# A transformer layer in float32: the FFN's first strip is entered token half by token half

## The chip, the cores and the metric

The kernel runs on one core of a Trainium2 chip. It issues work to five engines, each of which takes its instructions strictly in order: TensorE (PE in the profile; its weight loads are PEld), VectorE (DVE), ScalarE (ACT), GpSimd (POOL) and SyncE (SP), which issues nearly all DMAs. The metric is the device time of one execution in microseconds, as the median of several runs.

## The reference

One layer (DEPTH 1) of a hybrid diffusion backbone, D_MODEL 2048, over 256 latent tokens with 256 context tokens. A token mixer (gated DeltaNet, Fourier mixing and latent attention, merged by gates) is followed by one output projection and then by a dense SwiGLU FFN of hidden width 5632. Only the end of it matters here:

```
merged = merged + gates[:, :, i] * (branches[i] @ lp["w_branch"][i])
return merged @ lp["w_out"]
...
x = x + mod_l[:, 2] * _rms_norm(y_l, norm_g[l, 1])
h_l = _modulate(_rms_norm(x, norm_g[l, 2]), mod_l[:, 3], mod_l[:, 4])
x = x + mod_l[:, 5] * _rms_norm(_swiglu(h_l, w_ffn_in[l], w_ffn_out[l]), norm_g[l, 3])

def _swiglu(h, w_in, w_out):
    gu = h @ w_in
    return (jax.nn.silu(gu[..., :FF_HIDDEN]) * gu[..., FF_HIDDEN:]) @ w_out
```

All inputs are float32.

## The kernel before, in words

**Numbers.** Each operand of a large matmul is split into a high part, rounded to the matmul's reduced float32 format, and a low part, the rest. ScalarE writes the high part (`hi<-raw` for weights), VectorE or GpSimd the low part (`lo<-raw,hi`). A product is three matmuls (`mm3`, line 302): high x high, high x low, low x high, each 128 x 128 by 256 columns. Small products (`p<-...`) run in plain float32.

**Weights.** Every weight tile is 128 x 1024 (two k-tiles of 512 columns, 512 KB). `reserve` lists the tiles in order of use; `load_to` issues their DMAs into four buffers `raw`; `split_to` makes the high and low part in four pairs of buffers `hi`, `lo`; `get` hands a pair to the matmuls and asks for two tiles ahead.

**Order.** A planner (`Order`, line 100) writes every engine's instructions in an order that it finds from estimated costs: strips of matmuls (`job`) are steps that fill TensorE's time `pe_t`, and side work (`od.add`) is a generator that is taken up when its time is due. `yield 1.0` means: go on 1.0 us later. Background work on the modulation vectors (`bg_tick`, line 788, one step each `bgi` ns, not before `bgt`) is placed between. On the chip the engines keep to this order and wait for one another by semaphores.

**Output projection to FFN (lines 1685 to 1845).** `mT` is the merged branch output, transposed, in two parts. Strips 0 to 2 of `w_out` (512 columns) run token-major (`g_tm`: the tokens of a half are the output's partitions): each weight tile serves both token halves in turn. Strip 3 is cut in two of 256 columns; the second (`last_half`, line 1765) runs all of half 0 and then all of half 1. As soon as a half is done, its norm chain `x1_chain` (line 1728) is added: `rstd` of `y` (VectorE, and a power on GpSimd), the residual sum `y*rstd + x` in four pieces on VectorE, squares of it on ScalarE, a second `rstd`, the store `x1d<-y`, a diagonal `dr` with that `rstd`, and for four groups of four k-tiles (j = 0 to 3): float32 products `p<-dr,y` on TensorE (transpose and scale in one), modulation to `hs`, and the split of `hs` into `h` (high, ScalarE; low, GpSimd for half 0 and VectorE for half 1). For half 0 ScalarE does the modulation, for half 1 VectorE.

The FFN's 11 double strips (`ffn_in`, gate and up, 512 hidden columns) run feature-major (`g_fm`: hidden columns are the partitions, and all 256 tokens stream), so the first strip needs `h` of both halves for each k-tile. `to_hid` splits silu(gate) x up into `hid`, which the last projection `w_ffn_out` reads.

Of the kernel before, what the change touches and what calls it, by code (L numbers as in the profile page):

```python
# [9 lines left out]
F32 = mybir.dt.float32  # L10
# [37 lines left out]
BGI2 = 2700.0  # L48
BGI3 = 3000.0
LIM = 6000.0  # L50
# [195 lines left out]
def kernel(ctx, tc, x, c, ctx_in, c_ctx, w_ada, b_ada, norm_g, w_in, dn_conv, dn_a_log, dn_dt_bias,  # L246
# [52 lines left out]
    def wview(t, kt, n):  # L299
        return t[:, : kt * n].rearrange("p (a b) -> p a b", b=n)  # L300
# [41 lines left out]
    def split_to(i, must=0, eng=None):  # L342
        while wptr[1] < min(i, len(tiles)):
            j = wptr[1]
            load_to(j + 1)
            if j < must:
                od.pe_t = max(od.pe_t, raws[j][1].at)
            elif raws[j][1].at > od.pe_t:
                break
            _, kt, n, o = tiles[j]  # L350
            hi, lo = (wview(wp.tile([P, WE + 2 * FMS], F32R, tag=t, name=t)[:, o:], kt, n) for t in ("hi", "lo"))
            split(hi, lo, raws.pop(j)[0], eng)
            got[j] = (hi, lo, max(act.busy, (eng or dve).busy))
            wptr[1] += 1
            load_to(j + RAWB)
# [14 lines left out]
    for br in (1, 0, 2):  # L370
        for s in range(4):
            wb["br", br, s] = reserve(w_branch[br], 0, s * 512, 512, 8)
    for s in range(3):
        wb["o", s] = reserve(w_out, 0, s * 512, 512, KT)
    for s in range(2):
        wb["o", 3 + s] = reserve(w_out, 0, 1536 + s * 256, 256, KT, 4)
    for s in range(FF // 512):
        for u in range(2):
            wb["f", s, u] = reserve(w_ffn_in, 0, u * FF + s * 512, 512, KT, fm=True)
    for s in range(4):  # L380
# [1294 lines left out]
    job(load_rows, 2, G)  # L1675
    bx["mT"] = [yp.tile([P, KT, 256], F32R, name=f"mT{i}") for i in range(2)]
    y = yp.tile([P, 2, D], F32, name="y")
# [21 lines left out]

    mark(lambda: es_br.close())  # L1700
    for s in range(3):
        job(g_tm, wb["o", s], KT, 512, m_toks, ev_y(y, G, s * 512, 512, s))
    job(g_tm, wb["o", 3], KT, 256, m_toks, ev_y(y, G, 1536, 256, 3), kt=4)
    xr = {}
# [17 lines left out]
    x1d = dram.tile([P, 2, D], F32, name="x1d")  # L1722
    h2 = [hl.tile([P, KT, 256], F32R, tag=f"hl{i}", name=f"h2{i}") for i in range(2)]
    r2 = [None, None]
# [40 lines left out]
    def last_half():  # L1765
        lw = [get(wb["o", 4] + i, 0) for i in range(4)]
        ya = [acc(), acc()]
        ev = ev_y(y, G, 1792, 256, 4)
        for t in range(2):
            for kk in range(KT):  # L1770
                wh, wl = lw[kk // 4]
                mm3(ya[t][:, :256], mT[0][:, kk, tk[t]], mT[1][:, kk, tk[t]], wh[:, kk % 4, :], wl[:, kk % 4, :],
                    kk == 0, kk == KT - 1)
                if kk % 2:
                    yield
            ev(t, ya[t][:, :256])
            x1_done.append(od.add(x1_chain(t), 0.2))

    x1_done = []
    job(last_half)  # L1780
    od.drain()
# [5 lines left out]

    xh2 = [tuple(h2)]
    fx = {}
    es_sg = ExitStack()  # L1790

    def open_hid():
        es_yq.close()
        es_y.close()
        hp = ctx.enter_context(tc.tile_pool(name="hp", bufs=1, side="right", reuse_waits="tile"))
        fx["sgp"] = es_sg.enter_context(tc.tile_pool(name="sgp", bufs=2, reuse_waits="tile"))
        fx["hid"] = [hp.tile([P, NF, 256], F32R, name=f"hid{i}") for i in range(2)]
# [4 lines left out]
    def to_hid(s, sg):  # L1802
        yield 0.0
        hid = fx["hid"]
        split(hid[0][:, s * 4 : s * 4 + 4, :], hid[1][:, s * 4 : s * 4 + 4, :], sg)

    def ffn_in(s):
        if s == 0:
            for t in range(2):
                yield h2_in[t][0]  # L1810
        if s == 1:
            for _ in range(3):
                acc()
        box = []

        def ev_g(b, a):
            if b == 0:
                if s == 0:
                    open_hid()
                box.append(fx["sgp"].tile([P, 4, 256], F32, tag="sgf", name="sgf"))  # L1820
            act.activation(box[0][:, b, :], a[:, :256], AF.Silu)
# [7 lines left out]

        for kk, r in enumerate(g_fm(wb["f", s, 0], KT, xh2, ev_g)):  # L1830
            yield r
            if s == 0 and kk % 4 == 3 and kk < 15:
                for t in range(2):
                    yield h2_in[t][kk // 4 + 1]
# [135 lines left out]
```

## Time and profile before

| | us |
|---|---|
| three timed runs | 2012.37, 2017.92, 2030.83 |
| median | 2017.92 |
| profiled execution | 2000.15 |
| its span (first to last instruction) | 1998.3 |
| TensorE busy in the span | 1912.4 |
| VectorE, ScalarE, GpSimd busy | 1258.1, 912.9, 53.9 |

TensorE is the engine that sets the time. A difference of a few microseconds has to be looked for in the stretches in which it waits, or in which its matmuls take longer than elsewhere: the timeline of one engine gives, in brackets, how long the engine was idle before a row and who released it; the windows give each engine's busy time and the clock that TensorE was granted (1.00 is 2.4 GHz, 0.50 is 1.2 GHz). Output projection and step into the FFN lie at 1148 to 1280 us, the FFN's input strips end at 1744, the last projection fills the rest.

### The profile page before, as it was taken

The numbers are of one execution on the slowest core, as the hardware profiler recorded it, in microseconds if no ns is written. First come the engines' busy times: TensorE is split into PE (matmuls) and PEld (weight loads), VectorE is DVE, ScalarE is ACT, GpSimd is POOL, SyncE is SP. The second block draws the span as 40 slices with busy tenths as digits, with TensorE's granted clock in tenths as the row PEclk, the third lists the DMA queues.
The fourth block names the chain that finished last, engine by engine and source line by source line (L and its number), as shares of the span: only waits on it lengthen the run. The fifth ranks groups of instructions, "written<-read, shape, count | busy, mean of one in ns | idle before, by whom it ended". The sixth has DMA issues, their size and how long they took to land.

```text
span 1998.3 us, 41454 instructions
## 1 busy us (share of the span) xinstructions
PE 1912.4 (96%) x17359; PEld 1879.8 (94%) x17359; DVE 1258.1 (63%) x1891; ACT 912.9 (46%) x1492; POOL 53.9 (3%) x64
## 2 busy tenths in 40 slices
PE   5999989999999999999999999899999999999998
PEld 4899988999999899999999998899999999999998
DVE  3444758887866567656766876777755454554444
ACT  3213776564444345445444344544444444434442
POOL 1000010010000000000000000100000000000000
PEclk8999999999999899999999999899999999999999
DMA  9997667778998689855544887688876666676664
GB/s 298 290 291 190 229 185 230 262 227 256 310 306 267 198 289 292 277 167 176 161 146 135 293 285 274 222 299 278 273 218 197 191 196 194 180 269 194 193 195 141
DMA packets 310680, 463.45 MB, mean 232 GB/s; under 512 B 41224, under 2 KB 128670, under 8 KB 307805
## 3 DMA queue, kind: packets, MB, share of 16 engines
q1 hardware_dynamic: 310156, 459.81, 73.6%
q8 instruction: 136, 2.23, 0.5%
q0 software_dynamic: 336, 1.00, 0.2%
q14 instruction: 52, 0.42, 0.1%
HBM read 432.39 MB, written 28.35 MB: 231 GB/s over the span
## 4 chain that ended last, share of the span: by engine, by line
PE 49%; DVE 2%; ACT 1%; DMA 1%; issue 1%; POOL 0%; SPq 0%; DVEq 0%; POOLq 0%; ACTq 0%
PE acc L95 45%; PE p L95 4%; DMA raw<-in_w_ffn_out_dram 1%; ACT hi L95 0%; DVE lo L95 0%; DVE hs L95 0%; DVE aacc L95 0%; ACT hs L95 0%; DVE yo L95 0%; DVE dr L95 0%; DVE mg L95 0%; ACT h L95 0%; DVE yhl L95 0%; ACT sq L95 0%; POOL h L95 0%
## 5 line engine op out<-in xcount | busy, mean ns | idle before, releaser
L95 DVE TENSOR_TENSOR lo<-raw,hi 128x1024 fp32r<-128x1024 f32 (+2 forms) x534 | 648.8, 1219 | 464.6 <-ACT hi L95 459.6
L95 ACT ACTIVATE hi<-raw 128x1024 fp32r<-128x1024 f32 (+2 forms) x536 | 562.4, 1055 | 584.4 <-PE acc L95 462.2
L95 PE MATMUL acc<-h,hi 128*128 128x256 f32 x2816 | 481.3, 277 | 0.7 <-ACT h L95 0.4
L95 PEld LDWEIGHTS acc<-h,hi 128*128 128x128 f32 x2816 | 425.2, 188 | 1.3 <-ACT h L95 0.7
L95 PE MATMUL acc<-hi,hTl 128*128 128x256 f32 (+1 forms) x2112 | 413.0, 289 | 2.1 <-ACT ai L95 2.1
L95 PE MATMUL acc<-h,lo 128*128 128x256 f32 x1408 | 389.3, 277 | 0.7 <-DVE lo L95 0.7
L95 PEld LDWEIGHTS acc<-hi,hTl 128*128 128x128 f32 x2112 | 337.1, 191 | 2.9 <-ACT ai L95 2.5
L95 PE MATMUL acc<-lo,hTl 128*128 128x256 f32 (+1 forms) x1056 | 299.5, 284 | 0.0
L95 PEld LDWEIGHTS acc<-h,lo 128*128 128x128 f32 x1408 | 264.9, 188 | 1.0 <-DVE lo L95 1.0
L95 PE MATMUL acc<-hi,hid 128*128 128x256 f32 x1408 | 240.3, 276 | 0.5 <-ACT hi L95 0.5
L95 PEld LDWEIGHTS acc<-hi,hid 128*128 128x128 f32 x1408 | 211.9, 188 | 1.0 <-ACT hi L95 0.7
L95 PEld LDWEIGHTS acc<-lo,hTl 128*128 128x128 f32 x1056 | 201.8, 191 | 0.3 <-DVE lo L95 0.2
L95 PE MATMUL acc<-lo,hid 128*128 128x256 f32 x704 | 194.4, 276 | 0.9 <-DVE lo L95 0.9
L95 DVE SCALAR_TENSOR_TENSOR aacc<-araw,sc,aacc 128x512 f32<-128x512 f32 x240 | 179.3, 747 | 4.8 <-DMA araw<-in_w_ada_dram 3.7
L95 PE MATMUL acc<-hi,yhl 128*128 128x256 f32 x768 | 144.6, 285 | 7.1 <-DVE yhl L95 3.7
L95 PEld LDWEIGHTS acc<-lo,hid 128*128 128x128 f32 x704 | 132.2, 188 | 1.3 <-DVE lo L95 1.1
L95 PE MATMUL acc<-hTl,hi 128*128 128x256 f32 x640 | 125.4, 287 | 7.1 <-ACT kr L95 3.6
L95 PEld LDWEIGHTS acc<-hi,yhl 128*128 128x128 f32 x768 | 121.3, 191 | 8.9 <-DVE yhl L95 4.3
L95 PEld LDWEIGHTS acc<-hTl,hi 128*128 128x128 f32 x640 | 100.5, 195 | 10.7 <-ACT hi L95 4.0
L95 PE MATMUL acc<-lo,yhl 128*128 128x256 f32 x384 | 107.7, 281 | 0.0
L95 PE MATMUL acc<-hTl,lo 128*128 128x256 f32 x320 | 91.2, 285 | 1.2 <-DVE lo L95 1.2
L95 PE MATMUL acc<-hi,mT 128*128 128x256 f32 x512 | 89.5, 279 | 0.0
(306 smaller groups left out, 2517.5 us busy)
## 6 DMA issues: line engine op xcount, KB each, us to landing
raw<-in_w_in_dram SPq DMA_DIRECT2D x176, 512.0 KB
raw<-in_w_ffn_in_dram SPq DMA_DIRECT2D x176, 512.0 KB
araw<-in_w_ada_dram SPq DMA_DIRECT2D x148, 512.0 KB
raw<-in_w_ffn_out_dram SPq DMA_DIRECT2D x88, 512.0 KB
raw<-in_w_branch_dram SPq DMA_DIRECT2D x48, 512.0 KB
xt<-in_w_ada_dram SPq DMA_DIRECT2D x44, 512.0 KB
raw<-in_w_out_dram SPq DMA_DIRECT2D x32, 512.0 KB
hk<-qkvd SPq DMA_DIRECT2D x8, 1024.0 KB
```

The costliest lines, as they stand in the source:

```text
L95: return f(*a, **k)
```

## The change

Strip 3 of `w_out` is no longer cut: `last_o` runs its 512 columns for half 0 and then for half 1, and keeps its eight weight tiles for the second pass. Four of them lie in the four `hi`/`lo` pairs, the first four in buffers named `kept` in the space that `h` takes later (`hold`, in tags hl0, hl1). The FFN's first gate strip (`ffn_first`) runs token-major in the same way: all of half 0, waiting only for half 0's `h`, then all of half 1. Its tiles 0 to 3 lie in `hi`/`lo`, tiles 4 to 7 in `kept` buffers in the space of `mT`. A limit `wlim` lets a tile be refilled one tile behind the last use. The first up strip is token-major too; the product is transposed back (`turn_hid`, eight transposes) just before the last double strip. In `x1_chain` the delays are other, `dr` is made by ScalarE, modulation and low parts alternate between engines by j for both halves, and the store of `x1` is issued at the end. Background work is pushed back by 60 us at the step (`bgt`), and its spacing BGI3 is 2700 instead of 3000. The gated strip `sgf` has one buffer instead of two.

```diff
-BGI3 = 3000.0
+BGI3 = 2700.0
...
     def split_to(i, must=0, eng=None):
-        while wptr[1] < min(i, len(tiles)):
+        while wptr[1] < min(i, len(tiles), wlim[0]) or wptr[1] in held and wptr[1] < f0:
...
-            hi, lo = (wview(wp.tile([P, WE + 2 * FMS], F32R, tag=t, name=t)[:, o:], kt, n) for t in ("hi", "lo"))
+            if j in held:
+                hi, lo = (wview(v, kt, n) for v in held.pop(j)())
+            else:
+                hi, lo = (wview(wp.tile([P, WE + 2 * FMS], F32R, tag=t, name=t)[:, o:], kt, n) for t in ("hi", "lo"))
...
-    for s in range(3):
+    for s in range(4):
         wb["o", s] = reserve(w_out, 0, s * 512, 512, KT)
-    for s in range(2):
-        wb["o", 3 + s] = reserve(w_out, 0, 1536 + s * 256, 256, KT, 4)
...
+    o3, f0 = wb["o", 3], wb["f", 0, 0]
+    wlim[0] = f0
...
+    def hold(pool_, tags, j0):
+        kept = {}
+
+        def part(q):
+            if q // 2 not in kept:
+                kept[q // 2] = pool_.tile([P, 4 * WE], F32R, tag=tags[q // 2], name="kept")
+            v, o = kept[q // 2], q % 2 * 2 * WE
+            return v[:, o : o + WE], v[:, o + WE : o + 2 * WE]
+
+        for q in range(4):
+            held[j0 + q] = lambda q=q: part(q)
...
     def x1_chain(t):
         r = sum_rstd(ssy[:, t, :])
-        yield 1.0
+        yield 0.3
...
-        yield 0.0
+        yield -1.5
         r2 = sum_rstd(ssx[:, t, :])
-        od.dma(out=x1d[:, t, :], in_=y[:, t, :])
-        if t:
-            split_to(wb["f", 0, 0] + 2, eng=pool)
-        yield 1.0
+        yield 0.5
         dr = yp.tile([P, P], F32, tag=f"dr{t}", name="dr")
-        vmul(dr, ident, r2)
+        amul(dr, ident, r2)
         yield ada_in[3]
         yield ada_in[4]
+        bgt[0] = od.pe_t + 60000.0
         for j in range(4):
...
-                if t == 0:
+                if j % 2 == 0:
                     act.activation(o, i_, AF.Identity, bias=sh, scale=sc1)
...
-            split(h2[0][:, js, tk[t]], h2[1][:, js, tk[t]], hs, (pool, dve)[t])
+            split(h2[0][:, js, tk[t]], h2[1][:, js, tk[t]], hs, pool if j % 2 else dve)
             od.fire(h2_in[t][j])
             yield 0.0
...
+        od.dma(out=x1d[:, t, :], in_=y[:, t, :])
+
+    def last_o():
+        lw = []
         ya = [acc(), acc()]
-        ev = ev_y(y, G, 1792, 256, 4)
+        ev = ev_y(y, G, 1536, 512, 3)
         for t in range(2):
             for kk in range(KT):
...
+                i = kk // KC
+                if t == 0 and kk % KC == 0:
+                    lw.append(get(o3 + i, 3))
+                wh, wl = lw[i]
+                mm3(ya[t], mT[0][:, kk, tk[t]], mT[1][:, kk, tk[t]], wh[:, kk % KC, :], wl[:, kk % KC, :], kk == 0,
+                    kk == KT - 1)
+                if t and kk % KC == 1 and i >= 5:
+                    wlim[0] = f0 + i - 4
+                    split_to(f0 + 8, eng=pool if i == 5 else None)
+                yield
+            if t:
+                hold(yp, ("mT0", "mT1"), f0 + 4)
+                wlim[0] = f0 + 8
+            ev(t, ya[t])
+            split_to(f0 + 4 * t, f0 + 4 * t)
             x1_done.append(od.add(x1_chain(t), 0.2))
...
+    def turn_hid(t, sg):
+        pt = pst(t)
+        transpose4(pt, sg[:, t, :])
+        hid, ptv = fx["hid"], pt.rearrange("p (b t) -> p b t", b=4)
+        split(hid[0][:, 0:4, tk[t]], hid[1][:, 0:4, tk[t]], ptv)
+
+    def ffn_first():
+        lw = []
+        ga = [acc(), acc()]
+        for t in range(2):
+            for kk in range(KT):
+                i = kk // KC
+                if kk % 4 == 0:
+                    yield h2_in[t][kk // 4]
+                if t == 0 and kk % KC == 0:
+                    lw.append(get(f0 + i, 1))
...
+                if t and kk % KC == 1:
+                    wlim[0] = f0 + 8 + min(i + 1, 4)
+                    split_to(wlim[0])
+                yield
...
+        yield from g_tm(wb["f", 0, 1], KT, 512, [(h2[0], h2[1], s) for s in tk], ev_up)
...
+    job(ffn_first)
+    for s in range(1, FF // 512):
         job(ffn_in, s)
```

ScalarE's order before, at the norm of the two halves (`sq,ssy<-acc` closes a half's output strip, `sq,ssx<-y` are the squares of its residual sum, `hs` its modulation, `h` its rounding, `hi<-raw` a weight tile's high part; numbers tell the buffers apart):

```order
L95 ACTIVATE sq,ssx<-y 128x512 x4
L95 ACTIVATE sq,ssy<-acc 128x256
L95 ACTIVATE hs<-p_15221,modT 128x128 x4
L95 ACTIVATE h_13519<-hs 128x4x128
L95 ACTIVATE sq,ssx<-y 128x512 x4
L95 ACTIVATE hs<-p_15245,modT 128x128 x4
L95 ACTIVATE h_13519<-hs 128x4x128
L95 ACTIVATE hi<-raw 128x1024 x2
```

The same place after the change, on ScalarE (`kept<-raw` is the high part of a held tile, here tiles 4 to 6 of the FFN's first gate strip):

```order
L95 ACTIVATE hi<-raw 128x1024 x2
L95 ACTIVATE h_15172<-hs 128x4x128
L95 ACTIVATE hi<-raw 128x1024
L95 ACTIVATE sq,ssy<-acc 128x512
L95 ACTIVATE hi<-raw 128x1024
L95 ACTIVATE hs<-p_15245,modT 128x128 x4
L95 ACTIVATE h_15172<-hs 128x4x128
L95 ACTIVATE sq,ssx<-y 128x512 x4
L95 ACTIVATE h_15172<-hs 128x4x128
L95 ACTIVATE kept<-raw 128x1024 x3
L95 ACTIVATE dr<-cs,rstd 128x128
```

Half 1's closing square now stands behind three weight tiles' high parts, where it stood right behind half 0's squares; and the held tiles 4 to 6 stand behind the squares of half 1's residual sum and behind half 0's last rounding.

VectorE after the change, from the low part of half 0's first `h` on:

```order
L95 TENSOR_TENSOR h_15173<-hs,h_15172 128x4x128
L95 TENSOR_TENSOR lo<-raw,hi 128x1024
L95 TENSOR_SCALAR hs<-p_15206,modT 128x128 x4
L95 TENSOR_TENSOR lo<-raw,hi 128x1024
L95 TENSOR_TENSOR y<-acc,G 128x512
L95 TENSOR_TENSOR lo<-raw,hi 128x1024
L95 TENSOR_TENSOR h_15173<-hs,h_15172 128x4x128
L95 TENSOR_REDUCE ss<-ssy 128x1
L95 TENSOR_SCALAR rstd<-ss 128x1
L95 SCALAR_TENSOR_TENSOR y<-y,rstd,xr 128x512 x4
L95 TENSOR_SCALAR hs<-p_15312,modT 128x128 x4
L95 TENSOR_TENSOR kept<-raw,kept 128x1024 x2
```

Half 1's product with the gate, `y<-acc,G`, stands behind the low part of the FFN's tile 2, and its norm behind tile 3 and half 0's third `h`; before, nothing but half 0's own chain stood there.

TensorE just before the last double strip, after the change (`sgt` is the first strip's gated product):

```order
L95 MATMUL acc<-h_15172,lo 128x256
L95 MATMUL p_20426<-cs,sgt 128x128 x4
L95 MATMUL p_20433<-cs,sgt 128x128 x4
L95 MATMUL acc<-h_15172,hi 128x256
L95 MATMUL acc<-h_15173,hi 128x256
```

Before, no float32 product stood between the last `p<-dr,y` and the end of the FFN's input strips; now these eight transposes do.

## Rows read from the trace of the kernel before

**Rows 1.** Page: busy us and share of TensorE; chain that ended last, by engine.

```profile
PE 1912.4 (96%) x17359; PEld 1879.8 (94%) x17359; DVE 1258.1 (63%) x1891; ACT 912.9 (46%) x1492; POOL 53.9 (3%) x64
...
PE 49%; DVE 2%; ACT 1%; DMA 1%; issue 1%; POOL 0%; SPq 0%; DVEq 0%; POOLq 0%; ACTq 0%
```

**Rows 2.** Windows: length, busy PE, PEld, DVE, ACT, POOL, granted clock, DMA share, GB/s.

```profile
1205.00:1210.00 5.00, 5.00 (x46) 5.00 (x46) 3.34 (x5) 2.12 (x2) 0.00 (x0) 1.00 0.91 305
...
1245.00:1250.00 5.00, 1.78 (x10) 1.46 (x8) 2.19 (x5) 4.94 (x15) 1.28 (x1) 0.84 0.98 329
1250.00:1255.00 5.00, 0.46 (x2) 0.46 (x3) 2.38 (x2) 4.15 (x8) 4.69 (x4) 0.50 0.10 40
...
1260.00:1265.00 5.00, 5.00 (x32) 5.00 (x32) 2.81 (x6) 2.17 (x4) 1.27 (x1) 0.68 0.45 133
```

**Rows 3.** Timeline of TensorE at the step: start, length, operation, [idle before, releaser].

```profile
1239.37 0.28 PE L95 MATMUL acc<-hi,mT 128*128 128x256 f32 x1
1242.10 4.68 PE L95 MATMUL p<-dr,y 128*128 128x128 f32 x24 [2.45 <-DVE dr L95]
1254.54 3.78 PE L95 MATMUL p<-dr,y 128*128 128x128 f32 x16 [7.76 <-DVE dr L95]
1258.74 0.58 PE L95 MATMUL acc<-h,hi 128*128 128x256 f32 x1 [0.42 <-ACT h L95]
...
1265.65 1.06 PE L95 MATMUL p<-dr,y 128*128 128x128 f32 x8
1266.46 0.48 PE L95 MATMUL acc<-h,hi 128*128 128x256 f32 x2
...
1274.15 0.40 PE L95 MATMUL acc<-h,hi 128*128 128x256 f32 x2
...
1274.51 0.40 PE L95 MATMUL acc<-h,hi 128*128 128x256 f32 x2
...
1279.37 0.39 PE L95 MATMUL acc<-h,lo 128*128 128x256 f32 x1 [0.75 <-DVE lo L95]
```

**Rows 4.** Timeline of ScalarE at the step.

```profile
1234.10 0.38 ACT L95 ACTIVATE sq<-acc 128x256 f32<-128x256 f32 x1 [5.35 <-PE acc L95]
...
1245.11 0.63 ACT L95 ACTIVATE h<-hs 128x512 fp32r<-128x512 f32 x1
...
1248.10 1.47 ACT L95 ACTIVATE hs<-p,modT 128x128 f32<-128x128 f32 x4
...
1250.14 1.99 ACT L95 ACTIVATE hi<-raw 128x1024 fp32r<-128x1024 f32 x2
```

**Rows 5.** Timeline of VectorE at the step.

```profile
1242.18 2.74 DVE L95 SCALAR_TENSOR_TENSOR y<-y,rstd,xr 128x512 f32<-128x512 f32 x4 [0.23 <-POOL rstd L95]
...
1252.13 2.36 DVE L95 TENSOR_SCALAR dr<-cs,rstd 128x128 f32<-128x128 f32 x1 [2.11 <-POOL rstd L95]
...
1261.72 1.45 DVE L95 TENSOR_TENSOR lo<-raw,hi 128x1024 fp32r<-128x1024 f32 x1 [1.65 <-ACT hi L95]
1263.10 1.36 DVE L95 TENSOR_SCALAR hs<-p,modT 128x128 f32<-128x128 f32 x4
...
1266.10 1.23 DVE L95 TENSOR_TENSOR lo<-raw,hi 128x1024 fp32r<-128x1024 f32 x1 [0.25 <-ACT hi L95]
```

**Rows 6.** Timeline of GpSimd at the step.

```profile
1251.54 0.55 POOL L95 TENSOR_TENSOR rstd<-rstd,nhalf 128x1 f32<-128x1 f32 x1
1252.05 4.65 POOL L95 TENSOR_TENSOR lo<-raw,hi 128x1024 fp32r<-128x1024 f32 x2
...
1260.82 1.27 POOL L95 TENSOR_TENSOR h<-hs,h 128x512 fp32r<-128x512 f32 x1 [2.89 <-ACT h L95]
```

**Rows 7.** Timeline of TensorE, transposes in the output projection.

```profile
1154.69 0.60 PE L95 MATMUL p<-cs,mg 128*128 128x128 f32 x4
```

**Rows 8.** Windows of 50 us without a wait of TensorE.

```profile
500.00:550.00 50.00, 50.00 (x427) 50.00 (x426) 43.10 (x69) 21.84 (x27) 2.69 (x2) 1.00 0.96 308
...
1450.00:1500.00 50.00, 50.00 (x443) 50.00 (x443) 24.88 (x24) 21.62 (x24) 0.00 (x0) 1.00 0.73 221
```

More of the change, by code (lines that the diff above doesn't have):

```diff
@@ L320 @@
     wptr = [0, 0]
+    wlim, held = [1 << 30], {}
     def reserve(w, k0, c0, n, nk, kt=KC, fm=False):
@@ L1675 @@
     job(load_rows, 2, G)
-    bx["mT"] = [yp.tile([P, KT, 256], F32R, name=f"mT{i}") for i in range(2)]
+    bx["mT"] = [yp.tile([P, KT, 256], F32R, tag=f"mT{i}", name=f"mT{i}") for i in range(2)]
     y = yp.tile([P, 2, D], F32, name="y")
@@ L1698, with open_o @@
     m_toks = [(mT[0], mT[1], s) for s in tk]
-    mark(lambda: es_br.close())
-    for s in range(3):
+    def hold(pool_, tags, j0):
[7 more added lines that the diff above has]
+            held[j0 + q] = lambda q=q: part(q)
+    def open_o():
+        es_br.close()
+        hold(hl, ("hl0", "hl1"), o3)
+    mark(open_o)
+    for s in range(2):
         job(g_tm, wb["o", s], KT, 512, m_toks, ev_y(y, G, s * 512, 512, s))
-    job(g_tm, wb["o", 3], KT, 256, m_toks, ev_y(y, G, 1536, 256, 3), kt=4)
     xr = {}
@@ L1722 @@
     x1d = dram.tile([P, 2, D], F32, name="x1d")
-    h2 = [hl.tile([P, KT, 256], F32R, tag=f"hl{i}", name=f"h2{i}") for i in range(2)]
-    r2 = [None, None]
+    h2 = []
     h2_in = [[Event() for _ in range(4)] for _ in range(2)]
@@ L1760, in x1_chain @@
             js = slice(j * 4, j * 4 + 4)
-            split(h2[0][:, js, tk[t]], h2[1][:, js, tk[t]], hs, (pool, dve)[t])
+            if not h2:
+                h2.extend(hl.tile([P, KT, 256], F32R, tag=f"hl{i}", name=f"h2{i}") for i in range(2))
+            split(h2[0][:, js, tk[t]], h2[1][:, js, tk[t]], hs, pool if j % 2 else dve)
             od.fire(h2_in[t][j])
             yield 0.0
-    def last_half():
-        lw = [get(wb["o", 4] + i, 0) for i in range(4)]
+        od.dma(out=x1d[:, t, :], in_=y[:, t, :])
+    def last_o():
+        lw = []
         ya = [acc(), acc()]
-        ev = ev_y(y, G, 1792, 256, 4)
+        ev = ev_y(y, G, 1536, 512, 3)
         for t in range(2):
             for kk in range(KT):
[L1771 to L1776, printed above, removed]
+                i = kk // KC
[13 more added lines that the diff above has]
+            split_to(f0 + 4 * t, f0 + 4 * t)
             x1_done.append(od.add(x1_chain(t), 0.2))
     x1_done = []
-    job(last_half)
+    job(last_o)
     od.drain()
@@ L1786 @@
         return
-    xh2 = [tuple(h2)]
+    xh2 = []
     fx = {}
@@ L1805, in to_hid, with ev_up @@
         split(hid[0][:, s * 4 : s * 4 + 4, :], hid[1][:, s * 4 : s * 4 + 4, :], sg)
+    def turn_hid(t, sg):
[13 more added lines that the diff above has]
+                    lw.append(get(f0 + i, 1))
+                wh, wl = lw[i]
+                mm3(ga[t], h2[0][:, kk, tk[t]], h2[1][:, kk, tk[t]], wh[:, kk % KC, :], wl[:, kk % KC, :], kk == 0,
+                    kk == KT - 1)
+                if t and kk % KC == 1:
+                    wlim[0] = f0 + 8 + min(i + 1, 4)
+                    split_to(wlim[0])
+                yield
+        wlim[0] = 1 << 30
+        bgt[0] = od.pe_t
+        open_hid()
+        xh2.append(tuple(h2))
+        sg = fx["sgp"].tile([P, 2, 512], F32, tag="sgt", name="sgt")
+        for t in range(2):
+            act.activation(sg[:, t, :], ga[t], AF.Silu)
+        fx["turn"] = lambda: [turn_hid(t, sg) for t in range(2)]
+        def ev_up(t, a):
+            dve.tensor_tensor(out=sg[:, t, :], in0=sg[:, t, :], in1=a, op=ALU.mult)
+        yield from g_tm(wb["f", 0, 1], KT, 512, [(h2[0], h2[1], s) for s in tk], ev_up)
     def ffn_in(s):
-        if s == 0:
-            for t in range(2):
-                yield h2_in[t][0]
         if s == 1:
@@ L1813, in ffn_in @@
                 acc()
+        if s == FF // 512 - 1:
+            fx["turn"]()
         box = []
@@ L1828, in ev_up @@
                 od.add(to_hid(s, sg))
[L1830 to L1834, printed above, removed]
+        yield from g_fm(wb["f", s, 0], KT, xh2, ev_g)
         yield from g_fm(wb["f", s, 1], KT, xh2, ev_up)
-    for s in range(FF // 512):
+    job(ffn_first)
+    for s in range(1, FF // 512):
         job(ffn_in, s)
```

9 lines of the change are left out of this document (4 added, 5 removed).

## The prediction

> **What bounds the kernel now.** I read the page's busy shares first: TensorE is at work 96% of the span, and its matmuls are most of the chain that ended last [rows 1]. So only time in which TensorE waits, or runs at its lower clock, can be won. The windows show where that is at the place of the change: from 1245 to 1265 us the granted clock is between 0.50 and 0.84, while it is 1.00 at 1205 [rows 2]. The timeline of TensorE names the waits [rows 3]. The last matmul of the output projection ends at 1239.65 (1239.37 + 0.28); TensorE waits 2.45 us for the diagonal `dr` of token half 0, 7.76 for that of half 1, 0.42 for `h`, and 0.75 for a weight tile's low part at 1279.37.
>
> What does this step cost? From 1239.65 to 1279.37 are 39.7 us. In them stand the 8 groups of norm products, 0.81 us each at the full clock (1265.65 to 1266.46), so 6.5, and ten k-tiles of 12 FFN matmuls and two more, 122. One takes 0.113 us (50 us / 443 records [rows 8]), so 13.8. The loss is 39.7 - 20.3 = 19.4 us: 11.4 of waits and 8.0 of half clock (the groups of `dr` take 4.68 us for 24 records and 3.78 for 16, instead of 2.4 and 1.6), slower pace and hand-overs. These 19.4 us, 1.0% of the time, are all that the change can win there.
>
> **What the change removes.** The last 512 columns of `w_out` now run token half by token half, 96 matmuls or 10.9 us each instead of 5.4, so half 0's norm runs beside 10.9 us of matmuls. The first gate strip of the FFN also runs by halves, so that it can start before half 1's norm is done. If every cover held, the 19.4 us would go. I walk the new order from Z, the end of half 0's last output matmul, with durations from the rows.
>
> *Half 0.* Before, its chain takes 8.0 us from the square of its sums at 1234.10 [rows 4] to the first product at 1242.10 [rows 3]. In that time TensorE has 66 matmuls queued ahead of the first group, 7.5 us: it waits 0.5. Thirty matmuls (3.4) and three groups (2.4) later, at Z + 13.8, it enters the FFN.
>
> *First tile.* Scaling by ScalarE (1.47) and rounding (0.63) of the first four k-tiles end at Z + 11.0, the high part of the first FFN tile (1.0, half of 1.99) at 12.0 [rows 4]; its low part is on GpSimd, 2.33 (half of 4.65 [rows 6]), to 14.4. TensorE waits 0.6.
>
> *Third tile.* VectorE's order is: low part of tile 1, scaling of the second four k-tiles (1.36), low part of tile 2 (1.23) [rows 5]. VectorE's subtraction beside a GpSimd operation took 1.45 instead of 1.23, and one `dr` 2.36 beside the two GpSimd subtractions [rows 5, 6]. So I let tile 1 wait until GpSimd ends: 14.4 + 1.2 = 15.6; scaling to 17.0, rounding 17.6, high part of tile 2 18.6, low part 19.8. TensorE asks for it at 17.0: it waits 2.9. The Trainium skill, "SBUF — State Buffer", section "SBUF: two separate sides", says that the pair of ports that VectorE and GpSimd share is an exclusive lock, which also a VectorE operation with two SBUF inputs has to wait for; the rows agree (1.45 for 1.23). Without it, tile 1 would end at 14.2 and the wait would be 1.5: the sum would be 1.4 us less.
>
> *Fifth tile, the large one.* The square of half 1's sums stands on ScalarE behind the high part of tile 2, and its product with the gate on VectorE behind that tile's low part. So half 1's norm, whose matmuls end at Z + 13, begins at 19.8. Then come tile 3 (to 21.6), the third scaling and rounding (23.2), the root on GpSimd (0.55 [rows 6]; 24.2), four residual sums (2.74 [rows 5]; 26.9), the fourth scaling and rounding (28.9), and only then the high part of tile 4, whose turn on ScalarE is behind all of these: 29.9, the low part 31.1. TensorE is through with tile 3 at 23.4. It waits 6.5 and 1.2.
>
> *After it.* Tile 7 stands behind half 1's `dr`, scaling and rounding: 3.0. The last GpSimd subtraction of `h` costs 0.7. The waits are 0.5 + 0.6 + 2.9 + 7.7 + 3.0 + 0.7 = 15.4 us.
>
> *Clock.* Before, the clock fell to half after a wait of 2.45 us and again in one of 7.76, and came back some 8 us after work resumed [rows 2, 3]. A wait of 6.5 and one of 3.0 lie near these, so I expect it to fall again. I take the 8.0 us that were no wait before, less 2.3 for the first 24 records, whose slowness stood inside the 7.76: 5.7. The ends are 0 (no fall) and 8.0.
>
> *Added at the end of the FFN's input.* Eight transposes turn the token-major strip. Four took 0.60 [rows 7]: 1.2 us. Their two evacuations have a strip of 43 us ahead of their reader.
>
> *At nothing:* the 1 MB residual stores move behind the norm on SyncE's queue, and the data are read back only after the FFN; VectorE's `dr` goes to ScalarE (inside the 8.0). One buffer fewer for the gated strip: its reader is done some 7 conversions before the next strip writes; without that cover, each of ten strips would wait for one conversion, about 1 us. BGI3 of 2700 instead of 3000 and the pause of the modulation work by 60 us move VectorE work that has 450 us of FFN to finish in. The loads: 15 tiles in a row, four raw buffers. At 305 GB/s, the rate of the stage before [rows 2], a 512 KB tile takes 1.7 us, and tile 4's load has 14 us between the freeing of its buffer (Z + 14.4) and its turn.
>
> **Sum.** Removed 19.4; added 15.4 + 5.7 + 1.2 = 22.3; difference +2.9 us, with the bounds of the clock term and of the lock -4.2 to +5.2. The hand-overs in my walk are taken rather long, and I round to +2. The profiled execution took 2000.15 us, span 1998.3; by the sum it becomes 2002. The three timed runs lie 12 to 31 us above it, median 2017.92. So **2020 us**, likeliest range 2010 to 2030 with the spread of the runs. A difference of less than 1%, 20 us, can't be told from none here.
>
> **Rivals.**
>
> *The matmuls stay at the slower pace (slower).* After groups in another number format (`p<-cs`, `p<-dr`) the matmuls come at either of two spacings, at a clock of 1.00: 427 records in 50 us at one place, 443 at the other, 0.117 and 0.113 us [rows 8]. In the timeline the slower one (three matmuls in 0.36 us, 1274.15 to 1274.51) still holds long after the last `dr` group; behind the wait of 0.75 at 1279.37 the FFN is at the faster one [rows 3, 8]. After the change, 3720 matmuls follow the last group before the next one. If the spacing falls on the slow side, and no wait follows that resets it (my 0.7 is a weak one), they cost 3720 x 0.0042 = 16 us: 2036. For: the toss falls about evenly in this trace. Against: a wait follows in my walk. Chance 0.18. The Trainium skill, "TensorE: Matmul & The Clock Gate", section "Back-to-back issue gap", gives one spacing at the full clock, N / 2.4 + 2.5 ns, 109 ns for 256 columns. By that this rival does not exist and its 0.18 would go to the wash; the trace differs, with two spacings, both above it.
>
> *The waits are mostly hidden (faster).* If ScalarE and VectorE reach half 1's chain at its due time, the wait of 7.7 and the fall of the clock go: 2020 - 7.7 - 5.7 = 2007. For: the code asks for tiles at a time that a plan finds early enough. Against: engines work in order, and the rows before show ScalarE at 4.9 of 5 us in 1245 to 1250 [rows 2]. Chance 0.18.
>
> *The weights come late, so the halves step in on nothing held.* Then each of the eight first tiles waits for its load instead. Price: two or three loads of 1.7, 4 us more, 2024. Against: see the loads above. Chance 0.08.
>
> The wash keeps 0.56. The range for 8 in 10 reaches from the hidden case less the runs' spread, 2001, to the slow pace, 2036. Faster by over 1% (below 1998): a third of the hidden case's lower tail and little else, 0.07. Slower by over 1% (above 2038): nearly half of the slow pace, and a tail of the wash, 0.10. Within 1%: 0.83.
>
> **What would show it.** Right: TensorE waits for `dr` of half 0 under 1 us, enters the FFN without the wait of 7.76, and then waits 6 to 8 us at the fifth tile with ScalarE's high part as releaser, the clock at 0.50 for some windows, and 440 records per 50 us in the FFN. Wrong: a step with under 10 us of waits, a clock of 1.00 throughout it, or 425 records per 50 us.

## The result, and the profile after

The changed kernel takes 2021.31 us (median of 20 runs), the kernel before 2003.1 (20 runs beside them). The ratio is 1.0075, 95% interval 1.0054 to 1.0095: slower by 0.75%, some 15 us. The predicted time, 2020 us, is 1.3 us away, and that is luck: its base, the median of the three runs shown (2017.92), was 14.8 us too high, and the predicted difference, +2, was 13 us too small (16 by the medians, which lie 18.2 us apart). The three were among the six slowest of the 20. Over all its runs in this study the kernel before lies in two groups, near 2002 and near 2018 us; what speaks for a cause is shown below.

The profiled execution took 2008.61 us, span 2006.8, against 2000.15 and 1998.3 before. On the page of the changed kernel TensorE's share and the chain answer to [rows 1]: still 96% and half of the chain, with 12 us more of busy time.

```profile
PE 1924.5 (96%) x17367; PEld 1891.3 (94%) x17367; DVE 1258.2 (63%) x1887; ACT 912.7 (45%) x1489; POOL 53.6 (3%) x63
...
PE 49%; DVE 1%; ACT 1%; DMA 1%; issue 1%; POOL 0%; SPq 0%; DVEq 0%; POOLq 0%; ACTq 0%
```

TensorE's waits in the step into the FFN (1222 to 1285 us), grouped by who was waited for: total, times, longest.

```profile
PE acc L95 <- ACT kept L95: 7.4, 2, 5.6
PE acc L95 <- DVE kept L95: 1.8, 2, 0.9
PE acc L95 <- DVE lo L95: 1.1, 1, 1.1
PE acc L95 <- ACT hi L95: 1.0, 1, 1.0
PE acc L95 <- POOL lo L95: 0.3, 1, 0.3
```

That is 11.6 us; before it was 11.4 [rows 3]. The two waits for `dr` are gone, and waits of the same size for the FFN's weight tiles stand in their place. The timeline of TensorE after, which answers to [rows 3], has them one by one:

```profile
1221.04 0.39 PE L95 MATMUL acc<-lo,mT 128*128 128x256 f32 x1 [0.87 <-DVE lo L95]
...
1222.44 5.92 PE L95 MATMUL acc<-kept,mT 128*128 128x256 f32 x48
1228.19 0.29 PE L95 MATMUL acc<-hi,mT 128*128 128x256 f32 x1
...
1230.25 1.13 PE L95 MATMUL p<-dr,y 128*128 128x128 f32 x8
...
1237.05 0.39 PE L95 MATMUL acc<-lo,h 128*128 128x256 f32 x1 [0.29 <-POOL lo L95]
...
1241.02 0.39 PE L95 MATMUL acc<-hi,h 128*128 128x256 f32 x1 [0.99 <-ACT hi L95]
1242.51 0.39 PE L95 MATMUL acc<-lo,h 128*128 128x256 f32 x1 [1.10 <-DVE lo L95]
...
1251.93 0.58 PE L95 MATMUL acc<-kept,h 128*128 128x256 f32 x1 [5.58 <-ACT kept L95]
1253.42 5.27 PE L95 MATMUL acc<-kept,h 128*128 128x256 f32 x23 [0.90 <-DVE kept L95]
...
1262.90 0.39 PE L95 MATMUL acc<-kept,h 128*128 128x256 f32 x1 [1.77 <-ACT kept L95]
1264.16 0.86 PE L95 MATMUL acc<-kept,h 128*128 128x256 f32 x5 [0.87 <-DVE kept L95]
...
1279.87 0.29 PE L95 MATMUL acc<-hi,h 128*128 128x256 f32 x1
```

From the end of half 0's output matmuls (1222.44) to the end of the gate strip (1279.87) are 57.4 us. In them stand 288 matmuls (32.5 at 0.113) and eight groups of `dr` (6.5): a loss of 18.4 us where the kernel before lost 19.4. The step is a wash, as forecast. One price in it stood in no term: the 48 matmuls that stream a `kept` tile from 1222.44 to 1228.19 come 0.120 us apart, not 0.113.

What is new lies behind it. Windows of the changed kernel (columns as in [rows 2]), which answer to [rows 8]: two of 18 us in the first up strip, which is token-major, and in the second double strip, which is feature-major; two of 50 us later in the FFN and in `w_ffn_out`.

```profile
1282.00:1300.00 18.00, 18.00 (x161) 18.00 (x161) 11.81 (x13) 7.25 (x7) 0.00 (x0) 1.00 0.88 306
1303.00:1321.00 18.00, 18.00 (x155) 18.00 (x155) 12.76 (x15) 6.37 (x6) 0.00 (x0) 1.00 0.88 291
...
1650.00:1700.00 50.00, 50.00 (x427) 50.00 (x426) 24.57 (x23) 20.66 (x23) 0.00 (x0) 1.00 0.66 189
1800.00:1850.00 50.00, 50.00 (x444) 50.00 (x443) 24.00 (x21) 20.81 (x23) 0.00 (x0) 1.00 0.61 194
```

TensorE is busy for all of each window, at a granted clock of 1.00, and waits for nothing; yet 155 matmuls come in 18 us instead of 161, 427 in 50 instead of 444. The slow spacing begins at 1301.65, with the first feature-major matmul of the FFN, and lasts to the transposes at 1708.80: 3456 matmuls x (50/427 - 50/443 = 0.0042 us) = 14.6 us. A window also counts the matmuls that only reach into it, so this is a little low, as is every product with 0.0042 below: by their starts the 3456 came in 407.15 us, 0.1178 us apart, and the 192 of the up strip (1279.87 to 1301.65) 0.1134 apart, which makes 15.2 us. Busy shares and waits can't show this; the count in a window does.

The profiled executions differ by 8.5 us: 15.2 for the spacing, 1.5 for new waits in the last output strip (the 0.87 at 1221.04 and smaller ones), 1.0 for the transposes, -1.0 for the step, and -7.1 because the work ahead of all this took that much less in this execution (the matmul behind the same transposes of `mg` starts at 1132.97 instead of 1140.07). -1.1 is not assigned.

### The profile page after: what moved, and what is told of

It reads as the page before. It is cut to its first block, busy times and chain, and to the rows that moved or that the text cites. A ratio compares the mean times of both kernels' runs of the same rounds, so it can differ in the third digit from the quotient of the medians.

```text
span 2006.8 us, 41458 instructions
## 1 busy us (share of the span) xinstructions
PE 1924.5 (96%) x17367; PEld 1891.3 (94%) x17367; DVE 1258.2 (63%) x1887; ACT 912.7 (45%) x1489; POOL 53.6 (3%) x63
## 4 chain that ended last, share of the span: by engine, by line
PE 49%; DVE 1%; ACT 1%; DMA 1%; issue 1%; POOL 0%; SPq 0%; DVEq 0%; POOLq 0%; ACTq 0%
PE acc L95 45%; PE p L95 4%; DMA raw<-in_w_ffn_out_dram 1%; ACT hi L95 1%; DMA raw<-in_w_out_dram 0%; ACT hs L95 0%; DVE kept L95 0%; DVE hs L95 0%; DVE lo L95 0%; DVE y L95 0%; DVE yo L95 0%; DVE mg L95 0%; ACT h L95 0%; DVE yhl L95 0%; ACT kept L95 0%
## 5 line engine op out<-in xcount | busy, mean ns | idle before, releaser
L95 DVE TENSOR_TENSOR lo<-raw,hi 128x1024 fp32r<-128x1024 f32 (+2 forms) x527 | 641.3, 1222 | 472.0 <-ACT hi L95 470.1
L95 ACT ACTIVATE hi<-raw 128x1024 fp32r<-128x1024 f32 (+2 forms) x528 | 553.2, 1054 | 581.0 <-PE acc L95 478.7
L95 PE MATMUL acc<-h,hi 128*128 128x256 f32 x2560 | 450.7, 281 | 0.0
L95 PEld LDWEIGHTS acc<-h,hi 128*128 128x128 f32 x2560 | 394.4, 190 | 0.0
L95 PE MATMUL acc<-h,lo 128*128 128x256 f32 x1280 | 359.5, 281 | 0.0
L95 PEld LDWEIGHTS acc<-h,lo 128*128 128x128 f32 x1280 | 240.4, 188 | 0.0
L95 PE MATMUL acc<-hTc,hi 128*128 128x256 f32 x384 | 79.6, 290 | 5.9 <-ACT ai L95 5.9
```

What stands on the lines that cost most here:

```text
L95: return f(*a, **k)
```

## The experiments

Theory P: the loss is the slow spacing in the FFN, left behind by the step's last float32 products because no wait resets it. Theory S: the loss is the step itself, and the spacing a chance of one execution. The windows of 18 us above later gave theory R (roles): the slow spacing comes in where matmuls go over from token-major to feature-major without a pause. e11 and e12 test it. The times of e1 to e4 were taken beside the same runs of the kernel before, and so were those of e5 to e7, of e8 and e9, and of e11 and e12; between these sets, the ratios are what can be compared.

**e1_again**, the changed kernel untouched.

> The changed kernel once more, untouched, as the mark for the other three of this call. Theory P (pace): the loss of about 15 us against the kernel before lies in some 3700 FFN matmuls that come 0.0045 us further apart (0.118 for 0.113 us) because nothing behind the last float32 products of the step resets their spacing. Then this execution again has about 425 records per 50 us between 1300 and 1700 us, and 443 only behind the eight transposes near 1709. Theory S (step): the loss lies in the step itself (the waits of 5.86 and 2.05 us and the stretch at half clock), and the spacing of one profiled execution was a toss that comes out either way in another. Time by both: 1.0054 to 1.0095 of the kernel before, near 2018 us.

Measured: 2018.12 us, ratio 1.0040 (1.0010 to 1.0070). The FFN was slow again, and this time `w_ffn_out` too, which was fast in the first profile. A window of e1 there:

```profile
1850.00:1900.00 50.00, 50.00 (x426) 50.00 (x426) 23.44 (x20) 19.67 (x22) 0.00 (x0) 1.00 0.60 186
```

That is 1967 matmuls x 0.0042 = 8.3 us more, and this execution took 2029.62 us. In that stage the spacing comes out either way.

**e2_turn_early**, the same work with the float32 transposes 350 us earlier:

```diff
-        if s == FF // 512 - 1:
+        if s == 2:
             fx["turn"]()
```

> The changed kernel with its eight float32 transposes (p<-cs,sgt) at the start of the third double strip instead of the last; no work is added. P: the group throws the spacing over some 350 us earlier, so about 3080 more matmuls run at 0.113 us, 3080 x 0.0045 = 13.9 us less than the changed kernel, near 2004 us, and 443 records per 50 us from about 1370 us on. S: no change, within 2 us of the changed kernel, and 425 or 443 records per 50 us with no step at the transposes.

Measured: 2006.69 us, ratio 0.9983 (0.9958 to 1.0008), 11.4 us below e1, taken beside it. Windows of e2 ahead of the transposes (1357.86) and behind them:

```profile
1315.00:1333.00 18.00, 18.00 (x155) 18.00 (x154) 12.42 (x14) 6.86 (x7) 0.00 (x0) 1.00 0.87 284
...
1400.00:1450.00 50.00, 50.00 (x444) 50.00 (x443) 37.40 (x45) 23.17 (x25) 0.00 (x0) 1.00 0.87 288
```

The step's waits are those of the changed kernel, to 0.1 us. Moving eight small products took most of the loss away, so it is the spacing and not the step.

**e3_before_group**, the kernel before with a useless float32 group (`f32_group`: four `pe.transpose` of a constant):

```diff
         if s == 1:
             for _ in range(3):
                 acc()
+            f32_group()
```

> The kernel before with four float32 transposes of a constant (0.6 us, their result is read by nobody) at the start of the FFN's second double strip, where it is at the fast spacing. P: the group throws it to the slow one for the 3840 matmuls of ten double strips, 3840 x 0.0045 = 17.3 us, with the group's own 0.6 about 18 us slower than the kernel before (ratio 1.009), 425 records per 50 us up to 1744 us. S: 0.6 us slower, ratio 1.0003, 443 records.

Its profiled execution, 2024.07 us, was fast ahead of the group at 1316.04 and slow behind it:

```profile
1290.00:1315.00 25.00, 25.00 (x223) 25.00 (x222) 17.27 (x20) 12.89 (x15) 0.00 (x0) 1.00 1.00 343
1350.00:1400.00 50.00, 50.00 (x427) 50.00 (x427) 33.13 (x38) 21.37 (x23) 0.00 (x0) 1.00 0.82 263
```

But the median is 2006.35, ratio 1.0014 (0.9976 to 1.0053): 4 of its 12 runs lie at 2015.61 or above, 8 at 2010.98 or below. A miss for P: a float32 group can throw the spacing, as this execution shows, but the times do not show that it always does. (Of the kernel before's own 35 runs beside it, 8 lie above 2012.)

**e4_wait**, the changed kernel with one long wait and no float32 product:

```diff
+                if s == 1:
+                    wait_once(a)    # four copies on ScalarE, then a matmul that needs the last
```

> The changed kernel with one forced wait of TensorE and no float32 product: at the end of the second double strip four copies in a row on ScalarE (128 x 256 each, into a part of hid that is written over later), and one matmul in the large matmuls' own format that waits for the last. P, as the wait of 0.75 us reset the spacing in the kernel before: TensorE waits 1.2 to 1.8 us near 1364 us and then comes at 0.113 us, 3080 x 0.0045 = 13.9 less 1.5: 12 us faster than the changed kernel. P in a narrower form, that only float32 products throw the spacing: 1.5 us slower than the changed kernel, still 425 records behind the wait. S: 1.5 us slower.

Measured: 2017.85 us, ratio 1.0032 (1.0000 to 1.0064). TensorE of e4 waited 2.66 us and stayed slow, as the window behind shows:

```profile
1354.80 0.39 PE L95 MATMUL p<-hid 128*128 128x256 f32 x1 [2.66 <-ACT hid L95]
```

```profile
1400.00:1450.00 50.00, 50.00 (x427) 50.00 (x426) 36.35 (x44) 21.24 (x25) 0.00 (x0) 1.00 0.85 278
```

A wait does not by itself reset the spacing, and the premise of P in its wide form falls.

**e5_map**, `f32_group` at the start of each of nine double strips:

```diff
-        if s == FF // 512 - 1:
+        if s < FF // 512 - 1:
+            f32_group()
+        else:
             fx["turn"]()
```

> The changed kernel with four float32 transposes of a constant (0.6 us, read by nobody) at the start of each of the second to tenth double strips, so that one execution shows nine tosses. P: the spacing changes at these groups and nowhere between them. Counted over the six traces so far, a group of four threw slow matmuls to the fast spacing in 164 of 165 cases and fast ones to the slow in 132 of 208. So a slow strip (384 matmuls at 0.118 us) is always followed by a fast one (0.113), a fast one by a slow one about six times in ten; some four of the nine are slow: 2018 - 5 x 384 x 0.0045 = 8.6 + 9 x 0.6 = 5.4: 2015 us. S: 5.4 us more than the changed kernel, 2023, and one spacing throughout.

Measured: 2018.82 us, ratio 1.0049 (1.0017 to 1.0081), 4 us above P. Windows of 20 us, one in each of four double strips in a row:

```profile
1410.00:1430.00 20.00, 20.00 (x179) 20.00 (x178) 12.85 (x15) 9.35 (x12) 0.00 (x0) 1.00 0.85 287
1455.00:1475.00 20.00, 20.00 (x172) 20.00 (x171) 12.82 (x14) 8.64 (x11) 0.00 (x0) 1.00 0.79 262
1500.00:1520.00 20.00, 20.00 (x172) 20.00 (x172) 8.58 (x7) 8.90 (x12) 0.00 (x0) 1.00 0.64 184
1545.00:1565.00 20.00, 20.00 (x179) 20.00 (x178) 8.58 (x7) 9.66 (x12) 0.00 (x0) 1.00 0.64 185
```

Six double strips are fast (178 or 179), five slow (172 or 173), and every change falls at a group. With a group at the start of the second double strip, that strip was fast here, the only time. That a slow strip always turns fast failed: of four slow strips with a group behind them (the last of the four groups is the eight transposes) one turned fast.

**e6_step** shortens the step's waits, with the transposes early as in e2:

```diff
-                if j % 2 == 0:
+                if j % 2 == 0 or t == 0 and j == 1:
...
+        if t:
+            split_to(f0 + 6, f0 + 6)    # tiles 4 and 5, ahead of the four squares
+        for s in range(4):
+            ys = slice(s * 512, (s + 1) * 512)
             sq = yp.tile([P, 512], F32, tag="sq", name="sq", bufs=2)
```

> The changed kernel with the transposes at the third double strip (as in e2) and a shorter wait in the step: the fifth and sixth tile's conversions stand ahead of the four squares of half 1's residual sum on ScalarE (3.3 us by the trace after) instead of behind them, and half 0's second modulation is ScalarE's (idle there for 3.9 us) instead of VectorE's. If the wait of 5.86 us is ScalarE's queue, as its releaser says, it falls to 4 to 4.5, the wait of 2.05 at the eighth tile goes, and the whole is 3 to 5 us below e2: near 2003; up to 5 more if TensorE's clock then stays at 1.00 in the step. S, taken that the step is what made the change slow: the same 3 to 5 us. If the queue is not what holds the tile (its buffer or its load are): no change against e2.

Measured: 2001.94 us, ratio 0.9970 (0.9938 to 1.0001), 4.8 us below e2, and 5.3 below e7, which is nearly e2 and was taken beside it. ScalarE's order is what held the fifth tile. In the changed kernel:

```profile
1249.09 0.63 ACT L95 ACTIVATE sq<-y 128x512 f32<-128x512 f32 x1
...
1250.31 0.63 ACT L95 ACTIVATE h<-hs 128x512 fp32r<-128x512 f32 x1 [0.50 <-DVE hs L95]
1250.84 2.93 ACT L95 ACTIVATE kept<-raw 128x1024 fp32r<-128x1024 f32 x3
```

and in e6, where the conversion stands ahead of the squares and the wait left is for VectorE, 3.38 us:

```profile
1250.06 1.99 ACT L95 ACTIVATE kept<-raw 128x1024 fp32r<-128x1024 f32 x2
1252.66 0.63 ACT L95 ACTIVATE sq<-y 128x512 f32<-128x512 f32 x1 [0.60 <-DVE y L95]
```

```profile
1255.80 4.63 PE L95 MATMUL acc<-kept,h 128*128 128x256 f32 x24 [3.38 <-DVE kept L95]
```

The step's waits are 5.9 us in all instead of 11.6. The clock still fell (0.66 from 1255 to 1260 us in e6). The edit has two parts, and no run parts them.

**e7_nothing**, e2 with three parts undone that I had cost at nothing:

```diff
-BGI3 = 2700.0
+BGI3 = 3000.0
...
-        bgt[0] = od.pe_t + 60000.0
...
-        bgt[0] = od.pe_t
```

and the store of `x1` moved back ahead of `dr`.

> e2 (transposes early) with three parts of the change undone that the prediction cost at nothing: BGI3 3000 again, no pause of the modulation work at the step, and the residual store issued ahead of dr instead of at the end of the chain. By the prediction: no change against e2, within 2 us. Rival: without the pause, steps of the modulation work (0.74 us each on VectorE, and a float32 group of TensorE) fall into the step, where VectorE and ScalarE are what TensorE waits for: 2 to 5 us slower than e2, with aacc operations of VectorE between 1236 and 1265 us; and each further float32 group there is one more toss of the spacing.

Measured: 2007.20 us, ratio 0.9995 (0.9959 to 1.0031), 0.5 us from e2. The modulation work did come into the step, here on VectorE of e7:

```profile
1262.04 0.75 DVE L95 SCALAR_TENSOR_TENSOR aacc<-araw,sc,aacc 128x512 f32<-128x512 f32 x1
```

The wait at the fifth tile grew to 6.78 us while others fell. The three parts together are worth nothing that these runs can tell.

**e8_waits**, nine forced waits as in e4.

> The changed kernel with nine forced waits of TensorE and no float32 product: at the end of the second to tenth double strip two, three or four copies in a row on ScalarE, and one matmul in the large matmuls' format that waits for the last (about 1.5, 2.2 and 2.9 us). As the prediction had it (a wait resets to the fast spacing): 443 records per 50 us behind each wait from about 1364 us on. A wait is a toss like a float32 group: over the traces so far waits left slow matmuls slow in 6 of 12 cases and fast ones fast in 10 of 11, so most strips are fast behind the second or third wait, with changes at waits alone. Waits do nothing: 425 records per 50 us up to the transposes near 1740 us. Time: the changed kernel plus some 20 us of waits, less up to 12 us for the strips that are fast.

One run, 2044.19 us, 19.8 us of it in the nine waits. Windows of 30 us behind the second, third and eighth:

```profile
1420.00:1450.00 30.00, 30.00 (x257) 30.00 (x256) 18.77 (x20) 12.70 (x15) 0.00 (x0) 1.00 0.81 258
1470.00:1500.00 30.00, 30.00 (x267) 30.00 (x267) 18.13 (x18) 12.98 (x16) 0.00 (x0) 1.00 0.79 253
1700.00:1730.00 30.00, 30.00 (x267) 30.00 (x266) 13.56 (x12) 12.90 (x15) 0.00 (x0) 1.00 0.63 183
```

Slow behind the first two, fast from the third to the ninth; behind the ninth stand the transposes too, and the last double strip is slow. So a wait can turn the spacing, but of the three that met it slow one did, and none of the five that met it fast.

**e9_step_only**, e6 with the transposes late again.

> e6 with the transposes at the last double strip again: the shorter wait in the step without what throws the spacing. P: the FFN is slow again from the last float32 products of the step on, 3080 x 0.0045 = 13.9 us above e6, near 2016 us, 425 records per 50 us, ratio about 1.004. S (the step is the loss): as e6, near 2002 us.

Measured: 2010.60 us, ratio 1.0032 (1.0010 to 1.0054), 8.7 us above e6 (forecast 13.9) and 7.5 below e1, with 427 records per 50 us.

**e10_step_again**, e6 untouched.

> e6 once more, untouched, for a second interval against the kernel before, whose own runs lie in two groups (near 2002 and near 2018 us) that come in different numbers from call to call. P: e6's FFN runs fast behind the transposes in nearly every execution: median 1998 to 2005 us, no run above 2015, and a ratio of 0.995 to 1.000 to the kernel before, the lower the more of its runs are slow.

Measured: 1998.28 us, ratio 0.9943 (0.9908 to 0.9977), with 444 records per 50 us. One run, 2015.49, is above the bound I gave. By e6's interval and this one the version beats the changed kernel. Against the kernel before this interval alone is clear of 1, and 9 of that kernel's 17 runs beside it were above 2012. The medians of e1, e2, e9, e6 and e10 together (2018.1; 2006.7; 2010.6; 2001.9 and 1998.3; not all taken beside one another): the spacing is worth 9 to 12 us, the step's shorter waits 5 to 8.

**e11_switch** and **e12_no_switch**: the kernel before with 24 useless matmuls inside its third and seventh gate strip, in e11 with the roles of weights and `h` exchanged, in e12 as in the strip around them:

```diff
+        for q in range(4):    # e11: token-major
+            mm3(pt, xh[:, q, 0:P], xl[:, q, 0:P], wh[:, 1, :], wl[:, 1, :], True, True)
...
+        for q in range(4):    # e12: feature-major
+            for j in range(2):
+                bs = slice((2 * q + j) % 4 * P, (2 * q + j) % 4 * P + P)
+                mm3(pt[:, 0:256], wh[:, 1, bs], wl[:, 1, bs], xh[:, q, :], xl[:, q, :], True, True)
```

> The kernel before with 24 useless matmuls (2.7 us, no float32 product, no wait) in the FFN's third and seventh gate strip, in the token-major form: h stands still in TensorE and the weight tile streams, while the strip around them is feature-major. Theory R (roles): the slow spacing comes in where matmuls go over from token-major to feature-major without a pause. In the traces of the changed kernel's order the first up strip (token-major) is fast and the second double strip (feature-major) slow from its first matmul on, in nine of nine executions with nothing between the two, and matmuls that stream a kept tile are slow while those that stream hi and lo behind them are fast. The kernel before has no such seam in its FFN. So the FFN is slow (about 427 records per 50 us) behind the first block in every execution: 3456 x 0.0042 = 14.5 and twice 2.7 us above the kernel before's faster runs, near 2022 us, ratio 1.006 to 1.009, and no run below 2012. P in its first form (only float32 groups and waits throw the spacing): 5.4 us more, near 2009, ratio 1.0027, fast windows behind the blocks.

> The control of e11: the same 24 useless matmuls at the same two places in the form of the strip around them (feature-major: the weight tile stands still, h streams). R and P alike: 5.4 us more than the kernel before and no change of spacing at the blocks, ratio 1.0027, the same two groups of runs as the kernel before. If it turns slow as e11 does, it is any disturbance of the strip and not the roles.

e11 measured 2016.80 us, ratio 1.0037 (1.0002 to 1.0072). Windows of e11 ahead of the first block (1351), between the blocks, and behind the second (1538):

```profile
1300.00:1350.00 50.00, 50.00 (x444) 50.00 (x443) 35.14 (x40) 21.29 (x23) 0.00 (x0) 1.00 0.86 282
1400.00:1450.00 50.00, 50.00 (x426) 50.00 (x426) 34.62 (x40) 21.23 (x23) 0.00 (x0) 1.00 0.80 263
1600.00:1650.00 50.00, 50.00 (x444) 50.00 (x443) 25.40 (x24) 22.61 (x28) 0.00 (x0) 1.00 0.67 191
```

No wait, no float32 product: the block with exchanged roles threw fast to slow, and the second slow to fast. A timeline of e11 shows where; `p<-hi,h` begins a block of 24, `acc<-h,hi` is the first matmul behind it:

```profile
1351.29 0.28 PE L95 MATMUL p<-hi,h 128*128 128x256 f32 x1
...
1354.02 0.40 PE L95 MATMUL acc<-h,hi 128*128 128x256 f32 x2
...
1534.92 0.28 PE L95 MATMUL p<-hi,h 128*128 128x256 f32 x1
...
1537.75 0.40 PE L95 MATMUL acc<-h,hi 128*128 128x256 f32 x2
```

The first block takes 2.73 us, 0.114 a matmul, and the second 2.83, 0.118: each keeps the spacing of the strip ahead of it. The turn comes at the end of the block, where token-major goes over to feature-major as at the changed kernel's seam; going over the other way changed nothing. The FFN does not stay slow, as I had expected. If every block turns the spacing over, that gives, on 2002 and 5.4 for the blocks, 1536 x 0.0042 = 6.5 where the FFN was entered fast (2014) and 2566 x 0.0042 = 10.8 where slow (2018): all 12 runs lie between 2013.72 and 2022.11, in one group. e12 measured 2013.07, ratio 1.0072 (1.0035 to 1.0109), in two groups, six runs from 2006.34 to 2010.72 and six from 2015.42 up; the forecast was 1.0027. The six short runs are what parts the two kernels: 2002 and 5.4 leave no room for an FFN turned slow, and e11 has no run like them. The profiled execution of e12 was slow from the FFN's start, and neither block changed it, so it shows nothing of what such a block does to the fast spacing:

```profile
1280.00:1330.00 50.00, 50.00 (x427) 50.00 (x426) 36.86 (x42) 22.31 (x24) 0.00 (x0) 1.00 0.93 313
1400.00:1450.00 50.00, 50.00 (x427) 50.00 (x427) 35.81 (x43) 21.73 (x24) 0.00 (x0) 1.00 0.83 265
```

Up to the first block e12 is the kernel before, with the same last wait (0.76 against 0.75 [rows 3]). So that kernel enters its FFN fast or slow: fast in its own profile, e3 and e11, slow in e12. Its two groups of runs, 16 us apart, fit that (4102 x 0.0042 = 17 us), but none of its own executions in the upper group was profiled. R holds for the seam: in the changed kernel the up strip is fast (161 in 18 us) and the second double strip slow, in nine of nine profiled executions with nothing at the seam (the first profile, e1, e2, e4, e6 to e10). No run takes the seam out of the changed kernel; nearest comes e5, with a float32 group on it, where the strip behind it was fast.

## Why the prediction was right and wrong

*The base.* 2020 came from a median of three runs, 2017.92, plus 2; in 20 runs it is 2003.1. The prediction saw these runs 12 to 31 us above the profiled execution and put that down to the spread of the runs. So two misses of nearly the same size, 14.8 us too much in the base and 16 too little in the difference, left 1.3 us: the time was right by luck. By the prediction's own signs it was half right: a fifth-tile wait of 6 to 8 us behind ScalarE (5.58 + 0.90) and the clock at 0.50 came as forecast, but so did its sign of being wrong, 425 records per 50 us in the FFN (427).

*The step.* The walk held. It had the entry into the FFN at Z + 13.8 (measured 14.0, Z = 1222.44), a first wait of 0.6 (0.29), the third tile 2.9 (0.99 + 1.10), the fifth 6.5 and 1.2 (5.58, released by ScalarE's high part as forecast, and 0.90), the eighth 3.0 (1.77 + 0.87), the first `dr` 0.5 (none), the last `h` 0.7 (none): 15.4 in all against 11.6, hand-overs taken too long, as it said. The walk began too late, though, at Z: ahead of it TensorE now waits 1.5 us for the last tiles of `w_out`, and that stood in no term.

*The lock.* VectorE's low part of tile 1 beside GpSimd's subtraction took 2.56 us where one alone takes 1.23; first GpSimd, then VectorE of the changed kernel:

```profile
1234.62 2.38 POOL L95 TENSOR_TENSOR lo<-raw,hi 128x1024 fp32r<-128x1024 f32 x1 [4.88 <-ACT hi L95]
```

```profile
1235.52 2.56 DVE L95 TENSOR_TENSOR lo<-raw,hi 128x1024 fp32r<-128x1024 f32 x1 [1.21 <-ACT hi L95]
```

It ends 1.08 us after GpSimd does: priced at 1.4, measured 1.3. The Trainium skill, "SBUF — State Buffer", section "SBUF: two separate sides", has this as an exclusive lock of the shared ports; these rows agree.

*The clock.* It fell again, in the wait at the fifth tile of the changed kernel:

```profile
1250.00:1255.00 5.00, 2.17 (x8) 1.87 (x9) 3.32 (x6) 3.47 (x4) 1.38 (x2) 0.50 0.12 9
1255.00:1260.00 5.00, 5.00 (x30) 5.00 (x29) 0.90 (x1) 0.67 (x2) 1.31 (x1) 0.62 0.95 359
```

The term was 5.7; the step's loss that was no wait is 18.4 - 11.6 = 6.8, and that holds slower spacing and hand-overs too.

*The step that failed* is the weighing of the first rival, the matmuls at the slower pace: the sum put the FFN behind the step at the fast spacing, at no cost. The rival's sign and its price were right (16 forecast, 15 in the trace). Its chance, 0.18, and its mechanism were not. It took float32 groups as what sets the spacing and a wait as what resets it; e4 and e8 show that a wait need not reset it, e12 that it can be slow behind one, and e11 that going over from token-major to feature-major can turn it with neither. The change puts such a seam into the FFN, between the first up strip and the second double strip, where the kernel before has none. The prediction had no term for it. Why a seam turns the spacing is open. The Trainium skill, "TensorE: Matmul & The Clock Gate", section "Back-to-back issue gap", gives N / 2.4 + 2.5 ns, an estimate of 109 ns for 256 columns, for an isolated matmul; of a stream of weight loads and matmuls it says that both set the spacing. So its 109 ns was no argument against this rival in such a stream. Every trace of this case shows two spacings, 0.113 and 0.118 us.

*Costed at nothing*: store, BGI3 and pause, rightly as far as e7 can tell. The transposes cost 1.0 us of the 1.2 forecast, but their place also decides for how long the FFN stays slow (11.4 us between e1 and e2), and that stood in no term.

## What to carry to other kernels

Count the matmuls per window before and after a change, not only busy time and waits: the same instructions at a granted clock of 1.00 came about 4% further apart over 407 us, and nothing but the count showed it. Where a stream of matmuls changes which operand stands still, or follows float32 products, look at the spacing behind the seam in several executions; an early group of small products, as in e2, can be enough to turn it, though the same eight transposes left the slow spacing as it was in e4 and e5. A median of three runs of a kernel whose runs lie in two groups is no base for a difference of 1%.

## What the runs showed of the hardware

Matmuls in the reduced float32 format, 128 x 128 by 256 columns, have two spacings at a granted clock of 1.00, 0.113 and 0.118 us by their starts, and one held for up to 4149 in a row (e12, from 1277 us, slow). Four kinds of event change it.

- Going over from token-major to feature-major without a pause: fast to slow nine times of nine at the seam and once in e11, slow to fast once in e11. Going over the other way, into e11's two blocks, changed nothing.
- Another buffer: in all ten traces of the changed kernel's order, token-major matmuls that stream a `kept` tile come 0.119 to 0.120 us apart at that clock, also behind matmuls at 0.113, and those that stream `hi` and `lo` behind them come at 0.113 from the fourth on, with no wait, no float32 product and no change of roles between them (1222.44 to 1228.19 above).
- A wait: either outcome. Behind a wait of 0.75 us the kernel before went from slow to fast, and behind one of 0.76 e12 went from fast to slow.
- A float32 group. In the twelve traces up to e10, counting stretches of at least 12 matmuls on either side, groups of four records turned slow to fast in 332 of 336 cases, and fast to slow in 265 of 418. The second share hangs on the rule of counting: where no wait stands within 12 matmuls of the group, it is 51 of 136, and the first 76 of 78.

What in these events decides is open.
